# The second block's conditioning sums, moved beside the RWKV pairs, and a scratch tile moved to another ring

## The chip, the cores and the metric

One core of a Trainium2 chip runs the whole kernel. The metric is the device time of one execution in microseconds (us), lower is better. Engines are TensorE (PE, its weight loads PEld), VectorE (DVE), ScalarE (ACT), GpSimd (POOL) and SyncE (SP), which here only issues DMAs. Each works through its own queue strictly in order.

## The reference, cut to what matters

Two blocks run one after the other on 512 tokens of 2048 channels (with 256 context tokens in the first).

The first block normalizes and modulates its input, projects it with `w_in`, and sends half of the columns through a gated delta rule mixer with 8 heads and half through an RWKV-7 mixer with 16 heads, each in both directions of the sequence. The two outputs are joined and projected by `w_out`, scaled by a gate and added to the input.

Each block takes its shift, scale and gate from a conditioning vector:

```
shift, scale, gate = split(silu(c) @ w_ada + b_ada, 3)
```

`w_ada` is 2048 x 6144 for each block. The second block is `h = x*(1+scale)+shift`, a projection, windowed attention and a convolution branch, an output projection and a layer norm. Its shift and scale come from the first 4096 columns of `w_ada_2`. What the change moves is the product that gives the first block's gate (columns 4096 to 6143 of `w_ada`, stored as `w_ada_g`) and the second block's shift and scale (columns 0 to 4095 of `w_ada_2`): 6144 columns in all, each a sum over 2048 rows. These 6144 sums are called the conditioning sums here.

## The kernel before, in words

Matrix products are done as three products of rounded halves (`w_h`, `w_l` against `hxh`, `hxl`), so each weight tile `w_f` that SP loads is split by ScalarE (`w_h`, L274) and by GpSimd or VectorE (`w_l`, L275), with 3 slots for `w_f` and 2 for each half.

A list scheduler lays out the queues of all engines ahead of time from the order in which the program is written, priorities and an estimate of durations; a tile pool gives slots and makes an instruction wait for the release of its slot.

The stages in order of time are: modulation and the low-rank columns; 8 delta rule heads; 8 RWKV *pairs* of heads; the output projection; the second block. The RWKV stage works as a pipeline over the pairs p = 0 to 7. Each has these steps, all traced at a high priority:

- `rwkv_keys(p)`: keys, decay scans and Gram matrices (`rpg`, L1065),
- `rwkv_lanes(p)`: a triangular solve on VectorE, 30 dependent pairs of instructions (`rT` L745, `rL` L746) after four transposes (L1080),
- `rwkv_rest(p)` and `rwkv_levels(p)`: transposes and the merging of the solved blocks,
- `rwkv_chain(p)`: 12 dependent steps; each ends in one VectorE instruction (`GS`, L1214) that is put into the list `states`,
- `rwkv_out(p)`: group-norm (`gmean` L981, `rosq` L984, `gvar` L985), the gate `rzt` loaded from DRAM, and the store into `y_scr`.

Beside pair p, at a normal priority, TensorE streams the projection of pair p + 2 (`rwkv_proj`, matmuls at L394). Its results go through a ring of two [128 x 512] slots, the tag `mix` of the pool `r0`: `mr`, `mk`, `mv`, `mzth`, `mz`, each stored to DRAM. The group-norm scratch `rosq` and the gate `rzt` share one slot of their own in the pool `rp`.

After pair 5 nothing is left to project, and the *late stretch* begins (it is marked "fill out" in the program). Beside pairs 6 and 7 TensorE streams the first 13 of 16 k-tiles of the output projection (L1320), for 16 output tiles n. In the same place the conditioning sums are done, as 12 blocks of 512 columns (`ada_cols`). A block loads 16 tiles `awt` of [128 x 512] on SP (L1249), and VectorE multiplies each with one column of the activated conditioning vector and adds the block's sum so far, in place (`gate_sums`, L1252 for the first, L1254 for the 15 others). Then four matmuls with a column of ones (`pm`, L1266) sum over the partitions, and a copy (L1268) puts 4 columns into `ada`. The late blocks use six spare slots for `awt` and a PSUM bank of the projection's pool `mm` (2 banks). `ada` is first read when the rest of the output projection begins (L1361).

The program can already put blocks of 256 columns beside the pairs: the tuple `early` says how many behind each. It is empty before. `Beside` orders the sums of such blocks on VectorE: three behind each entry of the pair's `states`, and the rest behind the last.

In the last stage a sum of the same kind (`GateRow`, L1712) has a ring of four slots for its `awt`.

Of the kernel before, what the change touches and what calls it, by code (L numbers as in the profile page):

```python
# [10 lines left out]
FT = mybir.dt.float32  # L11
# [7 lines left out]
P = 128  # L19
D = 2048  # L20
KT = 16
NX = 512
# [182 lines left out]
def build(tc, a, dbg=None):  # L205
# [5 lines left out]
    with root:  # L211
# [13 lines left out]
        def vc(name, i=0, n=1):  # L225
            nm = next(v for v in vecs if name in VOFF[v])
            return vecs[nm][:, VOFF[nm][name] + i:VOFF[nm][name] + i + n]
# [7 lines left out]
        def rsqrt_pow(out, in_, n):  # L235
            G.tensor_tensor(out, in_, mh[:in_.shape[0]].to_broadcast([in_.shape[0], n]), op=OP.pow)  # L236
# [16 lines left out]
        mm = [actx.enter_context(tile_pool(name="mps", bufs=2, space=PSUM))]  # L253
# [193 lines left out]
        for i in range(4):  # L447
            px, pc = lx[i], lc[i // 2][:, i % 2]
            m = vc("mu", 24 + i)
# [11 lines left out]
        gps = gsb.enter_context(tile_pool(name="gps", bufs=2, space=PSUM))  # L461
# [433 lines left out]
        r0 = rsb.enter_context(tile_pool(name="r0", bufs=1, side="right"))  # L895
# [4 lines left out]
        rp = rsb.enter_context(tile_pool(name="r1", bufs=1))  # L900
        mm[0] = rsb.enter_context(tile_pool(name="mps2", bufs=2, space=PSUM))
        gps = rsb.enter_context(tile_pool(name="rps", bufs=2, space=PSUM))
# [68 lines left out]
        def rwkv_out(p, s):  # L971
            mark(f"r{p} out")
            po, bv = s["po"], s["bv"]
            oa = rp.tile([P, NX], FT, name="oa").rearrange("p (m h t) -> p m h t", m=4, h=2)
            oa8 = oa.rearrange("p m h t -> p (m h) t")
            po8 = po.rearrange("p m h t -> p (m h) t")
            mean = rp.tile([P, 8], FT, name="gmean")
            var = rp.tile([P, 8], FT, name="gvar")
            osq = rp.tile([P, NX], FT, name="rosq").rearrange("p (m t) -> p m t", m=8)
            bc8 = lambda t: t.rearrange("p (j o) -> p j o", o=1).to_broadcast([P, 8, 64])  # L980
            V.tensor_reduce(mean, po8, axis=AX.X, op=OP.add)  # L981
            V.tensor_scalar(mean, mean, 1.0 / 64, None, op0=OP.mult)
            V.tensor_tensor(oa8, po8, bc8(mean), op=OP.subtract)
            S.activation(osq, oa8, AF.Square)  # L984
            V.tensor_reduce(var, osq, axis=AX.X, op=OP.add)  # L985
            zt = rp.tile([P, NX], FT, name="rzt", tag="rosq")
            SY.dma_start(zt, mix_scr["z"][p])
            V.tensor_scalar(var, var, 1.0 / 64, 64e-5, op0=OP.mult, op1=OP.add)
            rsqrt_pow(var, var, 8)
            V.tensor_tensor(oa8, oa8, bc8(var), op=OP.mult)  # L990
            pt = cps.tile([P, 4, P], FT, name="rpto", tag="pU")
            for m in range(4):
                PE.transpose(pt[:, m, :], oa[:, m].rearrange("p h t -> p (h t)"), ident)
            yt = oa.rearrange("p m h t -> p (m h t)")
            S.activation(yt, pt.rearrange("p m t -> p (m t)"), AF.Identity, scale=vc("gn", p), bias=vc("gn", 8 + p))
            G.tensor_tensor(yt, yt, bv, op=OP.add)
            G.tensor_tensor(yt, yt, zt, op=OP.mult)
            S.dma_start(y_scr[8 + p], yt)
# [259 lines left out]
        def ada_cols(c0, n, wts, pool, tag, pace=ExitStack):  # L1258

            mark("fill ada")  # L1260
            b, sl = c0 // 512, slice(c0 % 512, c0 % 512 + n)
            w = a["w_ada_g"][b] if b < 4 else a["w_ada_2"][b - 4]
            acc = gate_sums(wts, lambda k: w[k, :, sl], cacts[:, min(b // 4, 1)], pace)
            pm = pool.tile([P, 4], FT, name="pm", tag=tag)
            for j in range(n // P):
                PE.matmul(pm[:, j:j + 1], acc[:, j * P:(j + 1) * P], cc("ones"), start=True, stop=True, skip_group_check=True)  # L1266
            ada_flat = ada.rearrange("p a k -> p (a k)")
            V.tensor_copy(ada_flat[:, c0 // P:(c0 + n) // P], pm[:, :n // P])  # L1268
# [9 lines left out]
                return tc.issue_after(states[min(i, len(states) - 1)])  # L1278

        start = []  # L1280
        early = ()
        for p in range(1, min(2, npairs)):
            rwkv_proj(p, r0, False, pace, tag="mix", bufs=2)
        with tc.high_priority(offset=4000):
# [1 line left out]
        for p in range(npairs):  # L1286
            start.append(len(slots))
            with tc.high_priority(offset=4000):
                rwkv_rest(p, now)
                rwkv_lanes(p, now)  # L1290
                nxt = rwkv_keys(p + 1) if p + 1 < npairs else None
                rwkv_levels(p, now)
                rwkv_chain(p, now)
                rwkv_out(p, now)
                now = nxt
            beside = Beside()
            for i in range(early[p] if p < len(early) else 0):
                ada_cols(256 * (sum(early[:p]) + i), 256, lambda k: rp.tile([P, 256], FT, name="awt", bufs=4), gps, "l", beside)
            if p + 2 < npairs:
                stream.n = min(stream.n, start[p])  # L1300
                rwkv_proj(p + 2, r0, False, stream, tag="mix", bufs=2)
# [284 lines left out]
        for t in range(8):  # L1586
# [13 lines left out]
            for j in range(2):  # L1600
# [17 lines left out]
                m = at_.tile([P, 4], FT, name="m", bufs=2)  # L1618
# [168 lines left out]
```

## Time and profile before

| what | us |
|---|---|
| median of 3 runs | 3392.07 (3390.76 to 3399.92) |
| the profiled execution | 3378.85 |
| its span in the profile | 3377.1 |
| TensorE busy in the span | 3093.9 (92%) |
| VectorE busy | 2324.4 (69%) |
| ScalarE busy | 1303.7 (39%) |
| GpSimd busy | 952.6 (28%) |

Mean granted TensorE clock over the span: 0.924 of full speed. [...]

How to read the profile: busy time of an engine is summed from its instructions; matmuls are pipelined and their ends modelled, so a busy TensorE isn't one at its peak. A wait is put down to what released it last. The chain that ended last is followed back from a stretch's last instruction to what released each step.

### The profile page before, as it was taken

What the parts mean: (1) busy time and instruction counts of PE and PEld (TensorE: products, weight loads), DVE (VectorE), ACT (ScalarE), POOL (GpSimd) and SP (SyncE); (2) the same over time, 40 slices, a digit from 0 to 9 for tenths busy, and PEclk for the clock granted to TensorE, in tenths of its full rate; (3) what the DMA queues carried; (4) which work ended last, traced back from release to release, by engine and by line L of the source; (5) the groups of instructions that cost most, each with busy time, mean ns of one, the idle gap of its engine ahead of it and who ended that gap; (6) DMA issues with size and microseconds to landing.
All of it is one profiled execution on the core that took longest, in us unless ns stands there. A gap on an engine that the chain in (4) does not pass through costs nothing.

```text
span 3377.1 us, 53576 instructions
## 1 busy us (share of the span) xinstructions
PE 3093.9 (92%) x20464; PEld 2447.9 (72%) x20464; DVE 2324.4 (69%) x3996; ACT 1303.7 (39%) x2767; POOL 952.6 (28%) x794
## 2 busy tenths in 40 slices
PE   7798998999898989999999998989978999999996
PEld 4477887788776867677677776667656778877775
DVE  7977678776887254755646637797678997573577
ACT  5133443344333234435344342413233336573423
POOL 3644343344343232233223232523041000002001
PEclk9899999998999877999999978788989999999998
DMA  8522222222222221212112112568653322223764
GB/s 338 190 76 79 79 70 65 71 84 72 67 65 83 90 70 48 64 49 79 56 59 61 51 55 95 180 186 253 197 198 134 114 84 88 85 79 119 261 212 137
DMA packets 206265, 375.13 MB, mean 111 GB/s; under 512 B 21911, under 2 KB 52280, under 8 KB 202680
## 3 DMA queue, kind: packets, MB, share of 16 engines
q1 hardware_dynamic: 196384, 356.07, 32.9%
q10 hardware_dynamic: 9624, 15.64, 1.3%
q8 instruction: 160, 2.62, 0.3%
q14 instruction: 97, 0.79, 0.1%
HBM read 333.75 MB, written 37.88 MB: 110 GB/s over the span
## 4 chain that ended last, share of the span: by engine, by line
PE 55%; DVE 27%; issue 6%; DMA 3%; ACT 2%; POOL 1%; SPq 0%; DVEq 0%; POOLq 0%; ACTq 0%
PE mm L394 24%; PE po L1758 4%; PE mm L1477 4%; DVE L L746 3%; DVE DG L745 3%; PE rpg L1065 3%; DVE awt L1254 2%; DVE rT L745 2%; DVE rL L746 2%; PE pU L93 2%; DVE acc L587 2%; DMA awt<-in_w_ada 2%; DVE uc L1496 2%; PE mm L1320 2%; PE pl L1016 1%
## 5 line engine op out<-in xcount | busy, mean ns | idle before, releaser
L275 POOL TENSOR_TENSOR w_l<-w_f,w_h 128x512 fp32r<-128x512 f32 x380 | 535.8, 1412 | 1036.7 <-ACT w_h L274 962.3
L274 ACT ACTIVATE w_h<-w_f 128x512 fp32r<-128x512 f32 (+2 forms) x688 | 424.4, 618 | 785.4 <-PE mm L394 265.8
L394 PE MATMUL mm<-hxh,w_l 128*128 128x512 f32 x1472 | 621.5, 422 | 15.5 <-POOL w_l L275 10.0
L394 PE MATMUL mm<-hxh,w_h 128*128 128x512 f32 x1472 | 623.0, 423 | 11.9 <-ACT w_h L274 10.7
L394 PE MATMUL mm<-hxl,w_h 128*128 128x512 f32 x1472 | 606.8, 413 | 0.0
L394 PEld LDWEIGHTS mm<-hxh,w_l 128*128 128x128 f32 x1472 | 290.6, 197 | 77.8 <-POOL w_l L275 12.6
L394 PEld LDWEIGHTS mm<-hxh,w_h 128*128 128x128 f32 x1472 | 288.9, 196 | 74.2 <-ACT w_h L274 13.5
L394 PEld LDWEIGHTS mm<-hxl,w_h 128*128 128x128 f32 x1472 | 289.7, 197 | 61.0 <-issue 1.5
L275 DVE TENSOR_TENSOR w_l<-w_f,w_h 128x512 fp32r<-128x512 f32 (+2 forms) x308 | 219.4, 715 | 145.8 <-ACT w_h L274 144.0
L1254 DVE SCALAR_TENSOR_TENSOR awt<-awt,cacts 128x512 f32<-128x512 f32 x180 | 169.3, 940 | 30.0 <-DMA awt<-in_w_ada 19.6
L1496 DVE SCALAR_TENSOR_TENSOR uc<-up,vecs,uc 128x512 f32<-128x512 f32 x240 | 169.4, 747 | 2.2 <-ACT uc L1494 1.0
L394 PE MATMUL mm<-hch,w_l 128*128 128x256 f32 x512 | 153.9, 301 | 1.4 <-POOL w_l L275 1.3
L394 PE MATMUL mm<-hch,w_h 128*128 128x256 f32 x512 | 150.4, 294 | 0.0
L1065 PEld LDWEIGHTS rpg<-A,BK 64*128 64x128 f32 x1280 | 128.6, 217 | 27.7 <-issue 11.4
L394 PE MATMUL mm<-hcl,w_h 128*128 128x256 f32 x512 | 148.3, 290 | 0.0
L1065 PE MATMUL rpg<-A,BK 64*128 64x64 f32 x1280 | 138.1, 307 | 10.5 <-POOL BK L1051 6.8
L745 DVE TENSOR_TENSOR DG<-L 128x30 f32<-128x30 f32 (+14 forms) x240 | 135.2, 563 | 5.3
L746 DVE TENSOR_TENSOR L<-L,DG 128x30 f32<-128x30 f32 (+14 forms) x240 | 134.1, 559 | 5.4
L745 DVE TENSOR_TENSOR rT<-rL 128x30 f32<-128x30 f32 (+14 forms) x240 | 124.4, 518 | 6.7
L1203 ACT ACTIVATE UV<-pU 64x256 f32<-64x256 f32 x96 | 36.2, 377 | 235.0 <-PE pU L1201 223.9
L236 POOL TENSOR_TENSOR cv<-cv,mh 128x4 f32<-128x4 f32 x1 | 1.4, 1435 | 437.5 <-DVE cv L1564 437.5
L746 DVE TENSOR_TENSOR rL<-rL,rT 128x30 f32<-128x30 f32 (+14 forms) x240 | 117.2, 489 | 6.7
(483 smaller groups left out, 6749.3 us busy)
## 6 DMA issues: line engine op xcount, KB each, us to landing
w_f<-in_w_in SPq DMA_DIRECT2D x496, 256.0 KB, 3.0
awt<-in_w_ada SPq DMA_DIRECT2D x192, 256.0 KB, 3.5
wt<-in_w_ada_t SPq DMA_DIRECT2D x20, 1024.0 KB, 6.5
w_f<-in_w_out SPq DMA_DIRECT2D x80, 256.0 KB, 2.9
awt<-in_w_ada_g SPq DMA_DIRECT2D x64, 256.0 KB, 3.6
wk<-in_w_ada_s SPq DMA_DIRECT2D x16, 768.0 KB, 6.0
w_f<-in_w_out_a SPq DMA_DIRECT2D x48, 256.0 KB, 3.6
lth<-lora_scr SPq DMA_DIRECT2D x32, 288.0 KB, 3.1
```

Source lines behind the costliest of these rows:

```text
L93: i = self.tc.nc.tensor.matmul(out, lhsT, rhs, start=first is None, stop=True, skip_group_check=True)
L274: S.activation(wh, raw, AF.Copy)
L275: lower[0].tensor_tensor(wl, raw, wh, op=OP.subtract)
L394: PE.matmul(po[:, :n], w_[:, k, :], h_, start=(kt == 0 and i == 0), stop=(kt == KT - 1 and i == 2))
L587: V.scalar_tensor_tensor(acc[:, :n], raw[:, j:j + n], cw(j), acc[:, :n], op0=OP.mult, op1=OP.add)
L745: V.tensor_tensor(t, U[:, r, k:k + 1].to_broadcast([n, k, nc_]), U[:, k:k + 1, c].to_broadcast([n, k, nc_]), op=OP.mult)
L746: step = V.tensor_tensor(U[:, r, c], U[:, r, c], t, op=OP.add)
L1065: ticks[p, d, "gram"] = PE.matmul(pg[h][:, c], BK[hp_, c0 + c, :, :], cols[hp_, c], start=True, stop=True, skip_group_check=True).ins
L1254: V.scalar_tensor_tensor(wt, wt, cvec[:, k:k + 1], acc, op0=OP.mult, op1=OP.add)
L1477: PE.matmul(po, w_[:, k, :], h_[kt], start=(kt == 0 and j == 0), stop=(kt == KT - 1 and j == 2))
L1496: V.scalar_tensor_tensor(uc[t], up[:, j:j + NX], cw(j), uc[t], op0=OP.mult, op1=OP.add)
L1758: PE.matmul(po[t], y_[kt][:, cols], w_, start=(kt == 0 and i == 0), stop=(kt == KT - 1 and i == 2))
```

## The change

Three edits. `early` becomes `(4, 4, 4, 4, 4)`: four blocks of 256 columns behind each of pairs 0 to 4, 20 blocks, which are 10 of the 12 blocks of 512. The late stretch keeps blocks 10 and 11. The early blocks get a ring of 2 slots for `awt` (the call that was there, never reached, asked for 4) and take their `pm` from the pool `mm[0]`, tag `mm`, instead of the pool of the chain, tag `l`. In `rwkv_out` the scratch `rosq` and the gate `rzt` give up their own slot and take slots of the ring `mix` (2 slots, pool `r0`).

```diff
@@ rwkv_out
-            osq = rp.tile([P, NX], FT, name="rosq").rearrange("p (m t) -> p m t", m=8)
+            osq = r0.tile([P, NX], FT, name="rosq", tag="mix", bufs=2).rearrange("p (m t) -> p m t", m=8)
...
-            zt = rp.tile([P, NX], FT, name="rzt", tag="rosq")
+            zt = r0.tile([P, NX], FT, name="rzt", tag="mix", bufs=2)
             SY.dma_start(zt, mix_scr["z"][p])
...
-        early = ()
+        early = (4, 4, 4, 4, 4)
...
             beside = Beside()
             for i in range(early[p] if p < len(early) else 0):
-                ada_cols(256 * (sum(early[:p]) + i), 256, lambda k: rp.tile([P, 256], FT, name="awt", bufs=4), gps, "l", beside)
+                ada_cols(256 * (sum(early[:p]) + i), 256, lambda k: rp.tile([P, 256], FT, name="awt", bufs=2), mm[0], "mm", beside)
             if p + 2 < npairs:
```

What it calls:

```python
        def gate_sums(wts, wsrc, cvec, pace=ExitStack):
            acc = None
            for k in range(KT):
                wt = wts(k)
                SY.dma_start(wt, wsrc(k))
                with pace():
                    if acc is None:
                        V.tensor_scalar(wt, wt, cvec[:, k:k + 1], None, op0=OP.mult)
                    else:
                        V.scalar_tensor_tensor(wt, wt, cvec[:, k:k + 1], acc, op0=OP.mult, op1=OP.add)
                acc = wt
            return acc
```

The number of late blocks follows from `early`, by lines that don't change (`na` counts the blocks):

```python
        na = n_early = sum(early) // 2
        for n in range(KT):
            while na < 12 and (na - n_early) * KT <= n * (14 - n_early):
                ada_cols(512 * na, 512, lambda k: hxp.tile([P, 512], FT, name="awt", tag=spare[k % 6]), mm[0], "mm")
                na += 1
```

## Rows read from the trace of the kernel before

**Rows 1.** Windows view: busy us (instructions) of each engine, granted clock, DMA share.

```profile
core 0: us, PE busy (x) PEld busy (x) DVE busy (x) ACT busy (x) POOL busy (x), PEclk, DMA share, GB/s
...
1681.00:1821.00 140.00, 133.40 (x1182) 99.50 (x1182) 80.57 (x131) 56.69 (x106) 41.45 (x31) 0.93 0.20 60
...
2098.00:2290.00 192.00, 162.69 (x1267) 126.22 (x1265) 164.01 (x228) 67.86 (x129) 74.75 (x51) 0.80 0.63 196
2290.00:2455.00 165.00, 157.22 (x1243) 122.62 (x1244) 108.47 (x156) 48.95 (x98) 31.80 (x24) 0.95 0.69 218
```

**Rows 2.** Chain that ended last, by line: 1681:1821, 2098:2290, 2290:2455.

```profile
by line: PE mm L394 23.6%; DVE rL L746 8.7%; PE rpg L1065 8.7%; issue 8.4%; PE pU L93 8.3%; DVE rT L745 7.1%; PE pU L1201 4.2%; PE pl L1016 3.8%; PE rpo L93 3.2%; PE rgv L1137 2.6%; PE rmx L1170 2.5%; PE rat L1132 2.4%; PE rpy L1155 2.3%; P
...
by line: DVE awt L1254 23.0%; issue 16.9%; DMA awt<-in_w_ada 6.8%; DVE rT L745 6.6%; DMA awt<-in_w_ada_g 6.1%; DVE rL L746 5.7%; PE mm L1320 4.4%; DVE rL L1080 4.1%; PE rmx L1170 3.4%; PE rpg L1065 3.3%; PE pl L1016 2.4%; DVE GS L1214 1.8%;
...
by line: PE mm L1320 26.1%; DVE awt L1254 23.2%; DMA awt<-in_w_ada 18.4%; issue 4.5%; PE pU L93 4.1%; PE rpg L1065 3.8%; PE pm L1266 2.4%; PE pU L1201 2.3%; DMA w_f<-in_w_out_a 2.1%; POOL w_l L275 2.0%; PE rpo L93 1.8%; PE rgv L1137 1.3%; D
```

**Rows 3.** Timeline of VectorE: start us, us, line, operation, tiles [idle before].

```profile
1323.17 0.43 DVE L1214 TENSOR_TENSOR GS<-pU,WC 64x256 f32<-64x256 f32 x1 [1.78 <-PE pU L93]
...
1764.85 0.18 DVE L745 TENSOR_TENSOR rT<-rL 128x30 f32<-128x30 f32 x1
...
1799.92 0.69 DVE L981 TENSOR_REDUCE gmean<-rpo 128x8 f32<-128x512 f32 x1
1800.52 0.69 DVE L839 SCALAR_TENSOR_TENSOR mz<-mzth,mm 128x512 f32<-128x512 f32 x1
...
1804.42 0.67 DVE L985 TENSOR_REDUCE gvar<-rosq 128x8 f32<-128x512 f32 x1
...
1809.77 0.19 DVE L746 TENSOR_TENSOR rL<-rL,rT 128x30 f32<-128x30 f32 x1
...
1939.79 0.68 DVE L981 TENSOR_REDUCE gmean<-rpo 128x8 f32<-128x512 f32 x1
...
2096.90 0.68 DVE L981 TENSOR_REDUCE gmean<-rpo 128x8 f32<-128x512 f32 x1
...
2210.63 0.18 DVE L745 TENSOR_TENSOR rT<-rL 128x30 f32<-128x30 f32 x1
2210.75 0.75 DVE L1254 SCALAR_TENSOR_TENSOR awt<-awt,cacts 128x512 f32<-128x512 f32 x1
...
2271.01 0.21 DVE L746 TENSOR_TENSOR rL<-rL,rT 128x30 f32<-128x30 f32 x1
```

**Rows 4.** Groups by line on VectorE, 2210.6 to 2271.1 us: busy us, mean ns.

```profile
L1254 DVE SCALAR_TENSOR_TENSOR awt<-awt,cacts 128x512 f32<-128x512 f32 x32 | 28.1, 878 | 1.7 <-DMA awt<-in_w_ada 1.6
...
L1252 DVE TENSOR_SCALAR awt<-awt,cacts 128x512 f32<-128x512 f32 x2 | 1.0, 481 | 0.0
```

**Rows 5.** Groups by line and form on VectorE, 1200 to 1300 us.

```profile
L957 DVE SCALAR_TENSOR_TENSOR k2r<-kmix,vecs_r,rpb 128x256 f32<-128x256 f32 x1 | 0.4, 424 | 0.0
```

**Rows 6.** Groups by line on VectorE, 2098 to 2455 us.

```profile
L1254 DVE SCALAR_TENSOR_TENSOR awt<-awt,cacts 128x512 f32<-128x512 f32 x180 | 169.3, 940 | 30.0 <-DMA awt<-in_w_ada 19.6 <-DMA awt<-in_w_ada_g 7.0
...
L1252 DVE TENSOR_SCALAR awt<-awt,cacts 128x512 f32<-128x512 f32 x12 | 7.8, 648 | 6.9 <-DMA awt<-in_w_ada 6.8
```

**Rows 7.** DMA issues of 1681 to 1821 us: KB each, median us to landing.

```profile
w_f<-in_w_in SPq DMA_DIRECT2D x16, 256.0 KB, 3.3
...
wup<-in_w_up SPq DMA_DIRECT2D x2, 48.0 KB, 1.8
```

**Rows 8.** Waits, 2098 to 2455 us: total us, times, longest us.

```profile
DVE awt L1254 <- DMA awt<-in_w_ada: 19.6, 22, 3.0
...
PEld pm L1266 <- DVE awt L1254: 7.5, 5, 3.6
DVE awt L1254 <- DMA awt<-in_w_ada_g: 7.0, 4, 2.6
DVE awt L1252 <- DMA awt<-in_w_ada: 6.8, 4, 2.2
```

**Rows 9.** Waits of the last stage, 3158 to 3290 us.

```profile
DVE awt L1712 <- DMA awt<-in_w_ada: 17.1, 21, 2.2
```

**Rows 10.** Waits of SP's own queue, 1681 to 1821 us.

```profile
SPq L264 <- POOL w_l L275: 71.4, 12, 15.2
```

## Prediction

> **What bounds the kernel now.** I first read the windows view, cut at the points where one pair's output begins. The reader should see two kinds of stretch. In a window of the steady pairs (1681 to 1821 us) TensorE is busy for 133.40 of 140 us at a mean granted clock of 0.93, and VectorE for 80.57 us [rows 1]. In the two windows that hold pairs 6 and 7, the projection of the first 13 k-tiles and all conditioning sums (2098 to 2455 us), TensorE is idle for 29.3 + 7.8 = 37.1 us, and the first has a clock of only 0.80 while VectorE is busy for 164.01 of 192 us [rows 1].
>
> Then the chain that ended last, for the same windows. In the steady pairs the work is shared between streamed matmuls (23.6%), the VectorE steps of the triangular solve (rL and rT, 15.8%) and many small TensorE groups; no conditioning sum exists there. In the late windows the sums (awt) and their loads hold 23.0 + 6.8 + 6.1 = 35.9% of 192 us and 23.2 + 18.4 = 41.6% of 165 us, that is 68.9 + 68.6 = 137.5 us of chain [rows 2]. So the sums do bound the late stretch, and taking most away must help there. What can be given back is not 5/6 of 137.5 = 115 us, since TensorE becomes the limit first.
>
> Last, the VectorE timeline, to see where sums land when they run beside a pair. One solve takes from 1764.85 to about 1809.96 us, 45.1 us, without sums; with them it takes from 2210.63 to 2271.22 us, 60.6 us [rows 3]. In that second solve 32 sums and 2 first products, 29.1 us, were slid between dependent steps [rows 4]. VectorE runs its queue in order, so a sum in front of a solve step delays it although it isn't needed for 200 us.
>
> **What is removed late.** Of 12 blocks of 512 columns, 2 stay late. If the late stretch ran like a steady pair, TensorE's idle share would be 6.6/140 = 4.7%, or 16.8 of 357 us instead of 37.1: 20.3 us back. Its clock in the first window would be 0.93 instead of 0.80, which on 162.69 busy us is 21.2 us. Together 41.5 us. At most all the idle time comes back and the clock stands at 1.00 in both: 37.1 + 0.20 x 162.69 + 0.05 x 157.22 = 77 us [rows 1].
>
> **What is added early.** 20 blocks of 256 columns, 4 behind each of pairs 0 to 4: 320 loads of 128 KB on SP and 320 VectorE sums, where 160 loads of 256 KB and 160 sums leave. A sum of 128x256 takes 0.43 us (the nearest instruction of the same kind and shape 0.424) [rows 5], against 0.75 where nothing disturbs it [rows 3] and a mean of 0.94 at 128x512 [rows 6]. So VectorE's work hardly changes: 320 x 0.43 = 138 us for 160 x 0.94 = 150 us.
>
> [...]
>
> The decisive edit is the ring of two. A sum writes into its own load's slot and reads the slot before it, so a slot comes free only when the next sum is done, and load k+2 can start only after sum k+1. With two slots no load is ever ahead: one step is a load and a sum in series. A load of 128 KB isn't in the trace; in the steady window 48 KB took 1.8 us to land and 256 KB 3.3 us [rows 7], a straight line between gives 2.4 us (estimate from these rows). With 0.43 and about 0.1 for the two handovers, a step is 2.9 us.
>
> [...]
>
> The sums of pair 0 can begin with its first state, at 1323.17 us, and pair 5's output begins at 2096.90 us [rows 3]: 774 us, or 267 steps of 2.9 us, 48 in each period of 140 us (output to output, 1799.92 to 1939.79 us [rows 3]). 53 sums spill into the late stretch. There remain 53 x 0.43 + 32 x 0.94 = 53 us of VectorE sums of 169.3 + 7.8 = 177 us (12 first products counted) [rows 6], 30%; so I take 70% of 41.5 us: **29 us gained**, between 15 and 77.
>
> The price in each of 774/140 = 5.5 periods has three terms.
>
> 1. In the solve. 45.1/2.9 = 15.5 sums fall into it. The late solve was lengthened by 15.5 us for 29 us of sums, a factor of 0.53, as a sum partly fills the gap between dependent steps [rows 3, 4]. 15.5 x 0.43 x 0.53 = 3.5 us; bounds 0 and 6.7.
> 2. VectorE standing before a sum whose load is late, with everything behind it (solve steps, state updates, group-norm). With the ring of six, 19.6 + 7.0 + 6.8 = 33.4 us in 30 waits over 192 loads: 0.17 us per load, 1.1 per late one [rows 8]. With a ring of four (the last stage) 17.1 us over 64: 0.27 [rows 9]. With two every load is late if VectorE arrives as planned. I take 0.4 us, nearer to the ring of four, because other work does stand between two sums. About 0.3 of the period is solve, where nothing hides it: 48 x 0.4 x 0.3 = 5.8 us; bounds 48 x 0.17 x 0.3 = 2.4 and 48 x 1.1 x 0.3 = 16 us.
> 3. TensorE, in order too, standing before the column matmuls (pm): 7.5 us in 12 blocks [rows 8], 0.6 each, 4 blocks: 2.5 us; bounds 0 and 5. The pm tile now takes one of the two banks of the streamed projection (mm); I count that in the upper bound.
>
> Together 12 us a period, 66 us in all. If VectorE's idle time (140 - 80.57 = 59 us, for 48 x 0.43 = 21 us of sums) hid all, it is nothing; with every upper bound 25 us a period, 138 us.
>
> **The scratch in the ring of the mixed streams.** rosq and rzt take both slots of a ring that holds mr, mk, mv, mzth and mz. They meet: mz is written at 1800.52 us while the squares are reduced at 1804.42 us [rows 3], so one may wait for the other's store, some 3 us. I count nothing: group-norm output isn't needed until the late stretch, and the next solve covers it. Without that cover it would be 3 us per pair, 24 us.
>
> **Sum.** The profiled execution took 3378.85 us (span 3377.1 and 1.75 around it), 13.2 us under the median of 3392.07. -29 + 66 = +37 us: 3416 for such an execution, **3429 us** as a median.
>
> **Rivals.**
>
> *Hidden (faster).* The sums fill VectorE's idle 59 us a period and no load is late: 2 us a period or so, 11 us, against 29 to 60 us back: 3343 to 3374, say 3360 us. For it: 59 us is nearly three times the need, and VectorE idles in long waits on TensorE. Against it: the sums in the late solve weren't kept to idle time [rows 3, 4]. It decides below 29/5.5 = 5.3 us a period. Chance 0.28.
>
> *A draw.* At 3.5 to 7 us a period cost and gain cancel within 10 us: 3392 us. Chance 0.10.
>
> *Lockstep through SP.* Loads of weights wait in SP's queue for slots, 71.4 us in 12 waits of one steady period, up to 15.2 us [rows 10], and with a ring of two a load of a sum behind such a wait stops VectorE, whose stop delays the matmuls that free the weights' slots. Two such waits of their mean, 6 us, on the path in each period add 12 us: 5.5 x 12 = 66 us more, 3495 us. Against it: SP's order was laid out with these waits in it. Chance 0.14.
>
> *The ring ends last.* At 3.6 us a step the 320 sums reach 1323 + 1152 = 2475 us, past the point where the columns are used, and end the stretch: about 3440 us or more. Chance 0.04.
>
> **How the numbers follow.** My forecast, 8 to 20 us a period, has 0.44. A change under 0.3% (10 us) can't be told from none here. Slower is 0.44 + 0.14 + 0.04 = 0.62, no change 0.10, faster 0.28. The range goes from 3345 us (hidden, with a gain of about 60) to 3500 us (lockstep); beyond it I leave the upper gain of 77 with no price, and every upper bound at once. The likeliest case by itself: 3405 to 3470 us.
>
> **What the changed profile would show.** Steady periods of about 152 us instead of 140, a solve of some 49 us with sums between its steps, VectorE waits on awt loads of 100 us or so in all, steps of 2.9 us, and fewer than 60 sums of 256 columns after pair 5; the late stretch some 29 us shorter with a granted clock near 0.9. I am wrong if the periods stay under 145 us (hidden), or if sums pass 2400 us (the ring ends last), or if SP's waits put single VectorE waits of over 4 us on the chain (lockstep).

## The result and the profile after

The change makes the kernel slower: 3792.45 us (median of 4 runs) against 3395.99 us of the kernel before on the same chip, a ratio of 1.117 (1.111 to 1.122), 396 us more. I had forecast 3429 us, 3345 to 3500.

The profiled execution took 3797.73 us, its span 3795.9, that is 418.8 more than the span before. Cut at the output of pair 5 (before 2096.90 us [rows 3], after 2423.63) and at the end of the streamed part of the output projection (before 2507.8, after 2928.5), the pairs up to 5 hold 326.7 us of it, the late stretch 94.0 (410.9 to 504.9), the rest -1.9. So both places where I placed a gain or a price are slower, the late stretch too.

First the page's slices: TensorE's busy share and granted clock, each digit 1/40 of the span (95 us).

```profile
PE   7898989999988887569595868988798899999997
...
PEclk9899999989988555758585868955599899999998
```

From the 14th slice on (1234 us) the clock falls to 5 and then swings, mostly between 5 and 8. (Before, it is low there too, 0.62 from 1234 to 1330 us, but back at 0.95 from 1330 to 1400.) Windows of two steady periods and of the late stretch, cut at the output of pair 7; the granted clock stands behind the busy times:

```profile
1810.00:2014.00 204.00, 156.43 (x1192) 123.76 (x1192) 104.08 (x193) 55.08 (x101) 38.87 (x28) 0.69 0.26 79
2014.00:2218.00 204.00, 151.28 (x1196) 118.62 (x1196) 112.37 (x202) 59.56 (x112) 44.87 (x32) 0.73 0.28 84
...
2424.00:2690.00 266.00, 235.00 (x2007) 184.21 (x2006) 158.18 (x267) 81.30 (x157) 42.52 (x30) 0.62 0.20 62
2690.00:2929.00 239.00, 205.44 (x787) 149.25 (x787) 54.45 (x78) 70.77 (x129) 89.30 (x74) 0.90 0.45 140
```

A period is 204 us instead of 140, and TensorE is idle for 48 to 53 us of it instead of 6.6 [rows 1]. VectorE is idle for 92 to 100 us, so its work isn't the bound. The chain that ended last, of the second of the two steady periods:

```profile
by line: DMA awt<-in_w_ada 40.8%; DVE awt L1254 11.9%; PE mm L394 10.4%; DVE rL L1080 3.7%; DVE rL L746 3.7%; issue 3.3%; DVE rT L745 3.2%; PE pl L1016 3.0%; DVE lth L1025 1.8%; PE pU L93 1.6%; PE pU L1201 1.4%; POOL gvar L236 1.3%; DVE Ga 
```

Where streamed matmuls led before (23.6%) and no sum was seen [rows 2], loads of sums and sums hold 52.7%, 107 us of 204. Twelve microseconds of VectorE's timeline in that period show how (start, duration, and in brackets the idle time before and what ended it):

```profile
2140.60 0.48 DVE L1254 SCALAR_TENSOR_TENSOR awt<-awt,cacts 128x256 f32<-128x256 f32 x1 [1.94 <-DMA awt<-in_w_ada]
2143.31 0.49 DVE L1254 SCALAR_TENSOR_TENSOR awt<-awt,cacts 128x256 f32<-128x256 f32 x1 [2.23 <-DMA awt<-in_w_ada]
2146.11 0.68 DVE L1254 SCALAR_TENSOR_TENSOR awt<-awt,cacts 128x256 f32<-128x256 f32 x1 [2.31 <-DMA awt<-in_w_ada]
2146.82 0.43 DVE L1214 TENSOR_TENSOR GS<-pU,WC 64x256 f32<-64x256 f32 x1
2149.04 0.48 DVE L1254 SCALAR_TENSOR_TENSOR awt<-awt,cacts 128x256 f32<-128x256 f32 x1 [1.79 <-DMA awt<-in_w_ada]
2151.74 0.49 DVE L1254 SCALAR_TENSOR_TENSOR awt<-awt,cacts 128x256 f32<-128x256 f32 x1 [2.22 <-DMA awt<-in_w_ada]
```

From sum to sum it is 2.7 to 2.9 us. VectorE stands for some 2 us before each, with everything behind it: the products that the chain step `GS` reads had ended on TensorE at 2145.84 us and VectorE was idle until 2146.11, but `GS` follows only behind the third sum, with no wait of its own. Three views say why: landing times of the 128 KB loads, SP's waits for slots in this period (total us, times, longest), and VectorE's waits for the loads of the early sums, from 1260 to 2424 us.

```profile
awt<-in_w_ada SPq DMA_DIRECT2D x126, 128.0 KB, 2.1
...
SPq L1249 <- DVE awt L1254: 118.5, 48, 9.5
...
DVE awt L1254 <- DMA awt<-in_w_ada: 217.0, 128, 4.1
DVE awt L1254 <- DMA awt<-in_w_ada_g: 149.9, 86, 3.7
DVE awt L1252 <- DMA awt<-in_w_ada: 5.8, 5, 2.3
DVE awt L1252 <- DMA awt<-in_w_ada_g: 5.0, 4, 2.2
```

The loads took 2.1 us (median) to land, and SP stood 118.5 us of this period before the next ones until a sum had freed a slot. Together VectorE waited 377.7 us in 223 waits, 1.18 us for each of the 320 early sums.

### The profile page after: what moved, and what is told of

Its sections match the earlier page's. It is cut to its first block, busy times and chain, and to the rows that moved or that the text cites. A ratio compares the mean times of both kernels' runs of the same rounds, so it can differ in the third digit from the quotient of the medians.

```text
span 3795.9 us, 54151 instructions
## 1 busy us (share of the span) xinstructions
PE 3259.7 (86%) x20464; PEld 2601.0 (69%) x20464; DVE 2319.1 (61%) x4166; ACT 1307.8 (34%) x2767; POOL 937.2 (25%) x794
## 4 chain that ended last, share of the span: by engine, by line
PE 44%; DVE 27%; DMA 13%; issue 5%; POOL 2%; ACT 2%; DVEq 0%; SPq 0%; POOLq 0%; ACTq 0%
PE mm L394 19%; DMA awt<-in_w_ada 7%; DMA awt<-in_w_ada_g 4%; DVE awt L1254 4%; PE po L1758 4%; PE mm L1477 3%; DVE DG L745 3%; DVE L L746 3%; PE pU L93 3%; DVE acc L587 2%; DVE rL L746 2%; DVE rT L745 2%; PE pU L1201 2%; DVE rL L1080 2%; PE mm L1320 1%
## 5 line engine op out<-in xcount | busy, mean ns | idle before, releaser
L275 POOL TENSOR_TENSOR w_l<-w_f,w_h 128x512 fp32r<-128x512 f32 x380 | 520.9, 1373 | 1270.0 <-ACT w_h L274 1223.1
L394 PE MATMUL mm<-hxh,w_l 128*128 128x512 f32 x1472 | 613.3, 417 | 11.1 <-POOL w_l L275 6.2
L394 PE MATMUL mm<-hxh,w_h 128*128 128x512 f32 x1472 | 612.1, 416 | 11.9 <-ACT w_h L274 10.7
L394 PE MATMUL mm<-hxl,w_h 128*128 128x512 f32 x1472 | 599.5, 407 | 0.0
L1254 DVE SCALAR_TENSOR_TENSOR awt<-awt,cacts 128x256 f32<-128x256 f32 (+1 forms) x330 | 190.1, 576 | 373.1 <-DMA awt<-in_w_ada 221.1
L394 PEld LDWEIGHTS mm<-hxh,w_l 128*128 128x128 f32 x1472 | 288.5, 196 | 74.5 <-DVE w_l L275 9.1
L394 PEld LDWEIGHTS mm<-hxh,w_h 128*128 128x128 f32 x1472 | 287.8, 196 | 74.1 <-ACT w_h L274 14.1
L394 PEld LDWEIGHTS mm<-hxl,w_h 128*128 128x128 f32 x1472 | 287.6, 195 | 59.8 <-issue 1.0
L1065 PE MATMUL rpg<-A,BK 64*128 64x64 f32 x1280 | 188.0, 394 | 99.5 <-DVE Ga L1067 66.7
L1065 PEld LDWEIGHTS rpg<-A,BK 64*128 64x128 f32 x1280 | 179.1, 300 | 112.9 <-DVE Ga L1067 70.2
L394 PE MATMUL mm<-hch,w_l 128*128 128x256 f32 x512 | 152.6, 298 | 1.4 <-POOL w_l L275 1.2
L394 PE MATMUL mm<-hch,w_h 128*128 128x256 f32 x512 | 149.4, 292 | 0.2 <-ACT w_h L274 0.2
L394 PE MATMUL mm<-hcl,w_h 128*128 128x256 f32 x512 | 147.0, 287 | 0.0
L1214 DVE TENSOR_TENSOR GS<-pU,WC 64x256 f32<-64x256 f32 x88 | 37.6, 428 | 145.3 <-PE pU L93 144.0
L1201 PE MATMUL pU<-GS,Ga 128*64 128x64 f32 (+1 forms) x768 | 95.4, 287 | 29.1 <-DVE GS L1214 18.8
L1201 PEld LDWEIGHTS pU<-GS,Ga 128*64 128x64 f32 (+1 forms) x768 | 76.3, 189 | 58.6 <-DVE GS L1214 28.2
```

The source lines that it names most:

```text
L275: lower[0].tensor_tensor(wl, raw, wh, op=OP.subtract)
L394: PE.matmul(po[:, :n], w_[:, k, :], h_, start=(kt == 0 and i == 0), stop=(kt == KT - 1 and i == 2))
L1065: ticks[p, d, "gram"] = PE.matmul(pg[h][:, c], BK[hp_, c0 + c, :, :], cols[hp_, c], start=True, stop=True, skip_group_check=True).ins
L1201: step = PE.matmul(pU[0:64, d, h], Ga[ks, d, step_chunk[d][i], h], GS[ks, i, d, h], start=True, stop=True, skip_group_check=True)
L1254: V.scalar_tensor_tensor(wt, wt, cvec[:, k:k + 1], acc, op0=OP.mult, op1=OP.add)
```

## The experiments

Letters in the expectations: **L**, the column matmuls of a pair stand ahead of the next projection in the line for the banks of `mm`; **S**, the scratch stands ahead of the projection in the line for the slots of `mix`; **R**, each late load of the ring of two adds its wait; **P** (formed later), the ring sets VectorE's pace. A *line* here is the order in which the program is written: a tile written earlier gets its slot earlier. All runs in one table, the ratio against runs of the kernel before on the same chip; the third column is the start of pair 5's output, the last the late stretch to the end of the streamed output projection. These two are from the one profiled execution of each run; that of the kernel before took 3378.85 us, 17 us under its median.

| run | us, ratio (95%) | pair 5's output | late |
|---|---|---|---|
| before | 3396 | 2096.9 | 410.9 |
| the change | 3792, 1.117 (1.111 to 1.122) | 2423.6 | 504.9 |
| e1 scratch alone | 3606, 1.060 (1.057 to 1.064) | 2160.5 | 576.3 |
| e14 scratch of pairs 0 to 5 alone | 3514, 1.035 (1.030 to 1.040) | 2168.2 | 476.6 |
| e11 the same, other order | 3398, 1.000 (0.997 to 1.002) | 2080.5 | 452.4 |
| e3 pm in another bank | 4013, 1.180 (1.174 to 1.186) | 2643.6 | 488.1 |
| e7 sums behind projection | 3756, 1.105 (1.100 to 1.109) | 2321.0 | 562.7 |
| e9 pm late | 3697, 1.087 (1.082 to 1.092) | 2323.8 | 502.8 |
| e10 sums, no scratch in the ring | 3729, 1.099 (1.092 to 1.105) | 2399.6 | 455.7 |
| e13 three orders mended | 3682, 1.084 (1.079 to 1.090) | 2364.3 | 453.6 |
| e18 e13 without loads | 3369, 0.991 (0.989 to 0.994) | 2124.3 | 375.5 |
| e15 e13, half the sums | 3436, 1.009 (1.007 to 1.012) | 2183.0 | 386.7 |
| e16 e13, ring of four | 3639, 1.070 (1.068 to 1.073) | 2388.8 | 372.6 |
| e23 e15, two a step | 3423, 1.006 (1.003 to 1.010) | 2148.9 | 405.9 |
| e24 e15, ring of four | 3423, 1.006 (1.003 to 1.008) | 2168.8 | 397.5 |

### The scratch

**e1**: the kernel before with the two edits of `rosq` and `rzt`, `early` empty.

> The kernel before with only the scratch moved: rosq and rzt in the ring mix, no early sums. Theory L (places in a ring are given in the order of the program's text, so the column matmuls' tile pm stands ahead of the projection of pair p + 2 in the ring of the two mm banks, and that projection waits for the sums): the scratch costs little, within 15 us of the kernel before. Theory R (the ring of two awt slots alone: VectorE stands before late loads): the same, within 10 us. Theory S (the scratch does it: rosq and rzt of pair p stand ahead of mr of pair p + 2 in the ring mix, so the projection cannot be stored before pair p's output): the steady periods grow from 140 towards 200 us, 3550 to 3750 us.

3606 us: the scratch that I had counted as nothing costs 208 us by itself. The windows view of one period, cut into four, first of the projection's matmuls (L394) alone, then its last quarter with all instructions:

```profile
1540.00:1579.00 39.00, 23.27 (x83) 16.23 (x83) 0.91 0.33 104
1579.00:1618.00 39.00, 19.31 (x71) 14.10 (x71) 0.88 0.23 75
1618.00:1657.00 39.00, 14.27 (x38) 8.96 (x38) 0.68 0.11 34
1657.00:1696.00 39.00, 0.00 (x0) 0.00 (x0) 0.50 0.00 1
...
1657.00:1696.00 39.00, 35.50 (x278) 25.98 (x279) 31.84 (x64) 5.81 (x13) 0.00 (x0) 0.50 0.00 1
```

The projection is done at the front of the period and none is left at its end. There TensorE is still busy for 35.50 of 39 us with the pair's small groups, at a granted clock of 0.50. SP's view of 1600 to 1800 us names the store that waits:

```profile
SPq L844 <- DVE mr L425: 53.4, 1, 53.4
```

SP stands 53.4 us before the store of `mr`, which can't be written before pair p's `rosq`, written ahead of it in the program, has had its slot and left it. At the output of pair 1 VectorE's reduction of `rosq` ends at 1543.98 us, and ScalarE's first write into `mr` starts at 1544.01:

```profile
1543.29 0.69 DVE L985 TENSOR_REDUCE gvar<-rosq 128x8 f32<-128x512 f32 x1 [1.24 <-ACT rosq L984]
...
1544.01 0.69 ACT L414 ACTIVATE mr<-mm,omu 128x512 f32<-128x512 f32 x1
```

**e14** gives the scratch of pairs 6 and 7 two of the six spare `awt` slots.

```diff
-osq = r0.tile([P, NX], FT, name="rosq", tag="mix", bufs=2)
+osq = (r0.tile([P, NX], FT, name="rosq", tag="mix", bufs=2) if p < 6 else hxp.tile([P, NX], FT, name="rosq", tag="hxl15"))
```

> The kernel before with the two scratch edits alone, no early sums, and for pairs 6 and 7 alone rosq and rzt take two of the six spare slots that the late awt have (the late awt keep four). So the scratch of pairs 0 to 5 stands in the ring of the mixed streams as in the change, that of pairs 6 and 7 doesn't stand ahead of the loads and stores (yf, pe) of the output projection. Theory S (the line of slots: who is written first in the program gets the slot first): of the 208 us that the scratch alone cost, about 63 us stood in pairs 0 to 5 (output of pair 5 at 2160 instead of 2097 us) and the rest in the late stretch, where the output projection no longer ran beside pairs 6 and 7. So this run takes 3396 + 60 = about 3460 us (3430 to 3490). Rival (the slots are merely held too long by the scratch, or the clock is lower for another reason): most of the 208 us stays, 3540 to 3610 us.

3514 us: 92 of the 208 us came from pairs 6 and 7, whose scratch stands ahead of `yf` and `pe` of the output projection, which in e1 started at 2423.0 us, behind the last pair, instead of 2119.9. The size was missed (3460 expected): 115 us remain, by the profiled executions 71 up to pair 5's output and 66 in the late stretch.

**e11** also writes the output of a pair behind the projection, with the same tiles and slots.

```diff
                 rwkv_chain(p, now)
-                rwkv_out(p, now)
-                now = nxt
+                if p + 2 >= npairs:
+                    rwkv_out(p, now)
+                cur, now = now, nxt
...
                 rwkv_proj(p + 2, r0, False, stream, tag="mix", bufs=2)
+                with tc.high_priority(offset=4000):
+                    rwkv_out(p, cur)
```

> As the run with the scratch of pairs 6 and 7 in spare slots, and also, for pairs 0 to 5, the whole output of pair p is written in the program behind the projection of pair p+2 instead of ahead of it. The ring, its two slots and the tiles in it are the same as in the change; only the order in the line differs. No early sums. Theory S: the projection of pair p+2 runs beside pair p again and the time returns to that of before, 3396 us, within 20 us. Rival (two slots are too few for nine tiles a pair instead of seven, whatever their order): 3440 us or more, no better than the run without this order.

3398 us, a ratio of 1.000: for pairs 0 to 5 two slots are enough, and the order in the line is the whole price; for pairs 6 and 7 it is gone with their place. The time lies otherwise, though: in the profiled executions pair 5's output comes 16 us earlier than before, and the late stretch, whose `awt` have four slots instead of six, is 41.5 us longer. The same two views of its period:

```profile
1530.00:1563.00 33.00, 14.58 (x48) 10.35 (x48) 0.90 0.33 98
1563.00:1596.00 33.00, 12.88 (x46) 8.02 (x46) 1.00 0.14 44
1596.00:1629.00 33.00, 12.33 (x41) 6.47 (x39) 1.00 0.21 65
1629.00:1663.00 34.00, 17.22 (x60) 10.65 (x60) 0.95 0.15 48
...
1629.00:1663.00 34.00, 30.84 (x239) 22.03 (x239) 32.11 (x57) 8.86 (x17) 7.47 (x5) 0.95 0.15 48
```

The projection lies evenly beside the pair again, and the last quarter runs at 0.95.

### The column matmuls and the bank

**e3** takes `pm` from the chain's pool (`gps`, tag `l`), **e7** writes the early sums behind the projection of pair p+2, **e9** stores each block's sum in DRAM and does its column matmuls in the late stretch, so that no early block needs PSUM.

```diff
 e3: -..., mm[0], "mm", beside)
     +..., gps, "l", beside)
 e7: ada_cols loop moved below rwkv_proj(p + 2, ...)
 e9: +            if pool is None:
     +                SY.dma_start(acc_scr[c0 // 256], acc)
     +                return
     ... and 20 times in the late stretch:
     +            SY.dma_start(acc, acc_scr[i])
     +            pm = mm[0].tile([P, 4], FT, name="pm", tag="mm")
```

> The changed kernel with pm taken from the banks of the chain (tag l) instead of the projection's (tag mm). Theory L: the line moves; now the transposes and products of the next pair (rat, rgv, rpy) stand behind four pm tiles, so the next pair's chain waits for the sums and a period is the 186 us of the sums and the part of the pair that follows them, 220 to 260 us: 3850 to 4100 us, worse than the changed kernel. Theory R and theory S: no change, 3750 to 3800 us.

> The changed kernel with two statements exchanged: the early sums of pair p are written after the projection of pair p + 2 instead of ahead of it. Nothing else differs. Theory L: the projection stands first in the line for the mm banks, and the sums of pair p hold back only the projection of pair p + 3, a pair later: the lag of the sums (64 steps of about 2.9 us, 186 us, against a period of 140) adds up over five pairs, less one pair of slack: 3500 to 3650 us. Theory R and theory S: no change, 3750 to 3800 us.

> The changed kernel, but the early blocks take no PSUM tile: each block's sum is stored to DRAM, and the 20 stored tiles are loaded again and given to the column matmuls in the late stretch. The sums, their ring of two and the scratch stay. Theory L: the projection of pair p + 2 runs beside pair p again, periods fall from 204 to 145 to 165 us, 3400 to 3520 us. Theory R: the waits of VectorE stay as they are (about 400 us in all), and so does the time, 3750 to 3800 us. Theory S: also 3700 to 3800 us.

e3 is 220 us slower than the change, as L wanted: `pm` in the chain's bank holds the chain itself (in the period from 1883 us ScalarE stands 68.3 us in one wait for the chain's `rat`, which has that bank). e9 takes 95 us off, e7 36. Neither is in L's range; e7 is where R and S put it, e9 is 3 us under S's range. Up to pair 5's output each takes some 100 us off, of which e7 gives 58 back in the late stretch. So L has a part, and the change's choice of bank is the better of the two, but neither comes near the kernel before. In the change's TensorE timeline the mechanism can be read: the first matmul of the projection of pair 2 comes right behind the last column matmuls beside pair 0, which waited for a sum.

```profile
1499.85 1.01 PE L1266 MATMUL pm<-consts,awt 128*128 128x1 f32 x4 [19.74 <-DVE awt L1254]
1500.73 0.77 PE L394 MATMUL mm<-hxh,w_h 128*128 128x512 f32 x1
```

The projections behind it do the same. That of pair 5 starts at 2115.0 us, 0.2 us behind the start of the last column matmuls and 101 us after an output; before, it is 35 to 42 us. The windows on its two sides:

```profile
2014.00:2115.00 101.00, 56.24 (x559) 49.80 (x559) 70.32 (x131) 28.84 (x54) 15.08 (x10) 0.57 0.17 53
2116.00:2187.00 71.00, 70.02 (x435) 51.93 (x434) 27.93 (x47) 20.04 (x37) 20.76 (x16) 0.96 0.44 124
```

TensorE is idle for 45 of the 101 us ahead of the projection, at a clock of 0.57, and for 1 of the 71 us with it.

### The sums by themselves

**e10** keeps all early sums and takes the scratch out of the ring. The squares overwrite the pair's output in PSUM, and `z` comes in four quarters through a small slot. **e13** is the change with three orders mended: e11's edits, and the early sums written between the projection and the output.

```diff
 e10
-            osq = r0.tile([P, NX], FT, name="rosq", tag="mix", bufs=2)...
+            osq = po8
...
-            G.tensor_tensor(yt, yt, zt, op=OP.mult)
+            for q in range(4):
+                sl = slice(q * P, (q + 1) * P)
+                zt = rp.tile([P, P], FT, name="rzt")
+                SY.dma_start(zt, mix_scr["z"][p][:, sl])
+                G.tensor_tensor(yt[:, sl], yt[:, sl], zt, op=OP.mult)
```

> All early sums as in the change, with their ring of two and their column matmuls in the projection's banks, but no scratch in the ring of the mixed streams: the squares are written back over the pair's output in PSUM, and the gate z is loaded in four quarters into a small slot of its own. Theory S: the 208 us of the scratch vanish, 3792 - 208 = about 3585 us (3550 to 3620), with the output projection beside pairs 6 and 7 again, and what remains over 3396 us is the line in the projection's banks and the ring of two. If the costs don't add up because both lines hold the same projection back (each alone is enough), it stays above 3680 us. My forecast of the change would want 3430 us here.

> The whole change, with three orders mended: scratch of pairs 6 and 7 in spare slots, output of pair p written behind the projection of pair p+2, and the early sums with their column matmuls written between the two, behind that projection. Ring of two, bank of the projection and all 20 early blocks stay. If the two lines of slots (mixed streams, and the projection's banks) are the whole cost, this gives 3345 to 3400 us: what the change takes from the late stretch shows. If the ring of two for the sums costs by itself (theory R, about 91 us from the run with late column matmuls), it gives 3440 to 3520 us. If neither order matters, 3700 us or more.

The parts don't add: e10 came out above 3680 us, as its expectation had it for that case, and e13 is in none of its ranges, 18 us under the one for "neither order matters". Without the scratch in the ring 330 us remain of 396, with three orders mended 283 (each against its own runs of before). e13 only moves the line for the bank by a pair: the projection of pair p+3 now stands behind the sums of pair p. In its trace each projection from pair 3 on still starts right behind a pair's last column matmuls, but the last three 31 to 34 us after an output, no later than before; yet its last three periods are 204 to 210 us. In e9, where that line is gone and the scratch's isn't, periods are 181 to 196 us. So theory L with S is not the whole cost. While early sums are done VectorE gets through 29 to 32 of them in each 100 us in the change, e7, e9, e10 and e13, and a pair has 64. That led to P: VectorE's queue is laid out ahead and was worked in that order (the `GS` behind the third sum above, 0.98 us after its input), so 64 sums stand between one pair's output and the next, and a period is at least 64 steps of the ring.

### What the loads do

**e18** is e13 with one tile, loaded once, read by all early sums; the 5120 early columns of its result are therefore not those of the reference.

```diff
+        fixed = rp.tile([P, 256], FT, name="awf")
+        SY.dma_start(fixed, a["w_ada_g"][0, 0, :, :256])
...
-                wt = wts(k)
-                SY.dma_start(wt, wsrc(k))
...
+                V.scalar_tensor_tensor(acc, fixed, cvec[:, k:k + 1], acc, op0=OP.mult, op1=OP.add)
```

> As the run with all three orders mended (3682 us), but the early sums load nothing: 320 sums of 256 columns, in the same places of VectorE's order, read one tile that was loaded at the start, so the early columns of the result are left out of the reference's and only VectorE's work and the column matmuls remain. Theories P and R: without loads there is no pace and no wait, only 64 x 0.43 = 28 us of sums in a period of VectorE with some 59 us idle: 3340 to 3420 us. Rival V (VectorE's own work between the solve's steps is the price): 3550 us or more.

3369 us, faster than before, with the same VectorE work in the same order. The loads, with the waits for slots that come with them, are the price: 313 us of e13's time. Without them the sums cost some 27 us up to pair 5's output, though the line for the bank is in the program as in e13.

**e15** has half the blocks, **e16** four slots of 128 columns.

```diff
 e15
-        early = (4, 4, 4, 4, 4)
+        early = (2, 2, 2, 2, 2)
 e16
+        early = (8, 8, 8, 8, 8)
-                ada_cols(256 * (sum(early[:p]) + i), 256, lambda k: rp.tile([P, 256], FT, name="awt", bufs=2), ...
+                ada_cols(128 * (sum(early[:p]) + i), 128, lambda k: rp.tile([P, 128], FT, name="awt", bufs=4), ...
```

> As the run with all three orders mended (3682 us), but with 2 early blocks behind each of pairs 0 to 4 instead of 4, so 10 blocks of 256 columns early and 7 of the 12 blocks of 512 late. New theory P (the ring sets the pace): VectorE's order is laid out ahead of time and holds all 64 sums of a pair before the next pair's last steps, and in every run with the ring of two a step takes about 3.2 us (31 to 34 sums in each 100 us), so a period can't be shorter than 64 x 3.2 = 205 us, which is what was seen; all other costs are hidden under it or not. Then 32 steps, 102 us, fit into a period of 132 to 140 us and nearly the whole price goes: 3360 to 3430 us. Rival R (each late load adds its wait of about 1.1 us to the path, wherever it falls): half the sums have half of the price of 286 us: 3540 us (3500 to 3580).

> As the run with all three orders mended (3682 us), same columns early and same bytes for the ring, but cut into four slots of 128 columns instead of two of 256: 40 blocks of 128 columns, 640 loads of 64 KB and 640 sums. Theory P: three loads are under way at a time, so a step takes about a third of a load and a sum, some (2.1 + 0.4) / 3 = 0.8 us, and 128 steps take 107 us, less than the period of 132 to 140 us: 3360 to 3460 us. Rival R (a wait of 1.1 us for each load): with twice the loads no better than 3682 us. If more and smaller instructions on VectorE and SP are themselves the price, 3600 us or more.

Half the sums have 35 of 283 us, an eighth and not the half that R wants; P's range is missed by 6 us. The ring of four gave 3639, where P wanted under 3460 and R no gain. It lies in the range of the third guess, that more and smaller instructions are themselves the price (3600 or more); e24 below, with 320 small sums for e15's 160, doesn't bear that out, but 640 without loads weren't run. Its windows, of the sums alone, from a pair's output to the first steps of the next chain, and over the rest of that chain and the solve:

```profile
1804.00:1905.00 101.00, 2.89 (x12) 3.11 (x12) 40.18 (x91) 0.59 0.33 93
1905.00:1984.00 79.00, 0.86 (x4) 0.83 (x4) 16.07 (x32) 0.92 0.28 83
```

91 sums in 101 us: the step fell from 3.2 us for 256 columns to 1.1 for 128, but they crowd between the chains, where the code puts all that go beyond three to a chain step. From a pair's output to the next chain's first step it takes 81 to 92 us here in pairs 1 to 4, before 59 to 65. I had compared 128 steps with the whole period; the pace holds by stretch. But that is 20 to 26 of the 56 to 69 us that these periods have grown by, and the line for the bank, which e16 has as e13 does, acts as well:

```profile
2099.02 0.59 PE L1266 MATMUL pm<-consts,awt 128*128 128x1 f32 x2 [2.16 <-DVE awt L1254]
2099.47 0.77 PE L394 MATMUL mm<-hxh,w_h 128*128 128x512 f32 x1
```

All five projections that stand behind early sums start like this, 100 to 110 us after an output, and end within 5 us of the next one. That is the division of the two windows above, with the low clock in the first. Crowded sums and the bank's line aren't parted by these runs; e16 with the column matmuls late would do it and wasn't run.

**e23** is e15 with two sums behind each chain step, **e24** has e16's ring, `early = (4, 4, 4, 4, 4)` blocks of 128, and four.

```diff
-                i = self.first + int(self.n / 3)
+                i = self.first + int(self.n / 2)      # e24: / 4
```

> As the run with half the sums (3436 us), but the order lets two sums stand behind each of the pair's last 11 chain steps instead of three, so 22 of 32 sums stand beside the chain and 10 behind it. Theory P, now by place: where sums stand, VectorE gets on at the ring's step of 3.2 us each. In the run with half the sums some 20 sums stood within the chain (20 x 3.2 = 64 us, the chain took 73 to 77 us instead of 60) and the rest between the chains (72 to 78 us instead of 60). Fewer sums for each step: the chain back to some 63 us, while the stretch between gets 3 to 6 us longer: 50 to 60 us less over five pairs at the chain and 15 to 30 us back: 3390 to 3420 us. Rival R (each late load costs the same wherever it stands): 3436 us within 10.

> The same half of the sums and the three mended orders, with a ring of four slots of 128 columns (the same bytes) and four small sums behind each chain step: 64 sums of 128 columns a pair. Theory P: with four slots a step took about 1.1 us in the run with the ring of four, so 44 sums beside the chain take 48 us of its 60 and 20 between the chains 22 of 60: the pairs keep periods of 131 to 145 us, the late stretch is 24 us shorter as in the run with half the sums, and the time is 3375 to 3395 us, at or a little under that of before. Rival R (0.43 us for each of 320 loads, from the run with the ring of four): 138 - 24 us more than before, about 3510 us.

Both 3423 us. R's 3510 for e24 is out, and P's 3375 to 3395 too; e23 lies between P's range (to 3420) and R's (from 3426) and doesn't tell them apart. Neither beats the kernel before. Up to pair 5 they are still 52 and 72 us longer than before, with VectorE idle for 103 and 41 us before loads of early sums. In e15 and e24 the solves of pairs 1 to 5 take 50 to 59 and 45 to 61 us, before 38 to 45; but in e23 they take 42 to 51, and it is no faster. Why half the sums keep a price of 9 to 13 us a period isn't settled by these runs.

## Why the prediction was wrong

The sign was right, the size was not, by 363 us. The sign proves little for my sum: the scratch, which I had counted as nothing, makes the kernel slower by itself (e1). Three steps failed, the price of the ring, the scratch and the bank of `mm`, and with them went the gain.

**The price of the ring of two.** The step itself held: 2.9 us predicted, 2.7 to 2.9 measured where sums follow each other, and 3.2 on average (204 us for 64). (Its 0.1 us for the handovers had no row of its own; only the whole step is measured.) What failed came after: "48 in each period of 140 us" and "53 sums spill into the late stretch". I let the sums fall where the ring allowed, as if they could be left over. They can't: VectorE's order is laid out ahead, 64 sums of a pair stand ahead of the next pair's output, and all early ones were done at 2314 us, before pair 5's output. From my own step the period should have been at least 64 x 2.9 = 186 us, 46 us over 140 instead of 12; e9's 181 to 196 us are near that, the change's 204 above it. The rival "the ring ends last" had this mechanism with the wrong consequence: I asked when the 320th sum ends, not what each pair waits for.

Then term 2 put 0.4 us for each load and counted only the 0.3 of the period that is solve. Measured are 1.18 us for each sum (my upper bound was 1.1), in every part of the period. "Where nothing hides it" was meant for the solve; it holds elsewhere too, as the chain step behind the third sum above shows: VectorE serves chain, keys, group-norm and the projection's evacuation from one queue. My 100 us of waits were 378. Term 1 didn't lengthen the solves: in steady pairs they take 37 to 39 us with 13 sums in each (15.5 forecast), where those of pairs 1 to 5 before take 38 to 45 (45.1 is the longest); but they hold 6 other VectorE instructions now instead of 12 to 14. My upper bounds of the three terms make 6.7 + 16 + 5 = 27.7 us a period and not 25, which is still too little.

e18 shows the loads as the cause (313 us) and e15 that it isn't a price for each load. That a ring of four with the same bytes helps by only 43 us (e16) stays open between the place of the sums and the bank's line. In the trace of before this could be read from rows that I had: 64 sums by the code, 2.9 us a step [rows 5, 7], the period [rows 3]. The load alone was put at 2.4 us, by the straight line between two rows [rows 7]; 2.1 were measured, so that was near enough, too.

**The scratch.** "I count nothing", with a bound of 24 us: by itself it costs 208 us (e1). I looked for a collision in time (`mz` against the squares, 3 us) and not for the order in which the tiles get their slots. Pair p's scratch is written ahead of the projection of pair p+2, which before ran beside pair p; so that projection had to wait for the end of the pair, and the clock fell to 0.50 where only small groups were left. For pairs 0 to 5 order alone undoes it, for pairs 6 and 7 another place does (e11). My cover, "the next solve covers it", was about the wrong waiter: not the group-norm's output was late but the projection behind its scratch.

**The bank of `mm`.** "I count that in the upper bound" of 5 us a period. It is a line like the scratch's: each projection stood behind the sums of a pair, some 100 us into the period, and without it (e9) the whole is 95 us shorter.

**The gain.** 29 us were forecast for the late stretch, and it became 94 us longer, where the output projection first started at 2696.4 us instead of 2119.9, behind the scratch of pairs 6 and 7. The scratch isn't all of it: in e10 and e13, where it is out of the way, the late stretch is still 45 and 43 us longer than before, and the output projection starts at 2500.0 and 2493.7, after the last projections of pairs, which end at 2472 and 2457 behind the last early sums. The gain shows only with the loads gone (e18, 35.4 us shorter), with the ring of four (e16, 38.3) or, smaller, with half the sums (e15 24, e24 13, e23 5). Against e11, whose late `awt` have four slots as theirs, it is 77 us in e18 and 80 in e16.

Of the rivals, lockstep through SP came nearest in time (3495), but its mark, single VectorE waits of over 4 us before sums, is seen once in 223 waits (4.1). Nor do weights come late behind the sums' loads in SP's queue: from 1323 to 2424 us ScalarE waits 10.7 us in 3 waits for `w_f`. No run put the sums' loads on another queue. "Hidden" and "a draw" are out. The periods passed 145 us, as I had said they would, but to 204 and not 152.

The parts, with both kinds of cost in one column: 3792 us with all; 110 off by mending three orders, the bank's by one pair (e13); 313 more off by taking the loads away (e18). They overlap: the scratch's 208 us alone shrink to some 64 when sums already slow the pairs (change against e10).

## What to carry to other kernels

When work is added to an engine with a fixed order, multiply its count in each stretch by its slowest step (here a load and a sum, with a ring of two) and compare with that stretch; here (64 x 2.9 = 186 us against 140) what didn't fit was not left over, it stretched the period, to 204 us. Before a tile moves into another ring, write down the line for its slots as the program is written, not as it runs: a tile of a late step, written early, held up all that stream behind it here (208 us in e1). After mending such an order, look in the trace whether the line is gone or has only moved by a step. Costs on the same stretch overlapped here (the scratch's 208 us alone, some 64 beside the sums), so each is measured alone and with the other mended.

## What the runs showed of the hardware

Work on TensorE that was nearly unbroken, as the profile models its ends, stood at a granted clock of 0.50 of full speed: in the last quarter of e1's period TensorE was busy for 35.50 of 39 us, with small groups alone. In that of e11, with 60 matmuls of 128x512 among them, it was busy for 30.84 of 34 us and got 0.95. The same small matmuls of the chain in the two (the last number before the idle time is the mean in ns):

```profile
L1201 PE MATMUL pU<-GS,Ga 128*64 128x64 f32 x64 | 8.9, 321 | 1.5 <-DVE GS L1214 1.2
...
L1201 PE MATMUL pU<-GS,Ga 128*64 128x64 f32 x36 | 3.2, 229 | 1.7 <-DVE GS L1214 1.7
```

So where the streamed matmuls were gone from beside the chain of small ones, the chain's matmuls were slower here, too: 321 ns for 229. And the whole period of e1:

```profile
1540.00:1696.00 156.00, 151.34 (x1182) 116.29 (x1183) 75.51 (x129) 55.06 (x104) 41.01 (x30) 0.74 0.17 54
```

TensorE is idle for 4.7 of 156 us, no more than before (6.6 of 140 [rows 1]), with as many instructions: the period is longer by the clock (0.74 for 0.93 [rows 1]), not by waiting.
